# Both FFN products by one level of Strassen's seven half-size products, in two phases with the gated result parked in DRAM

## The chip, the cores and the metric

The kernel runs on one core of a Trainium2 chip. Its time is the device time of one execution in microseconds (us); before the change it is 1385.53 us, the median of three runs (1383.79 to 1386.12).

## The reference

One layer of an encoder on 1024 tokens of width 1024, in float32: a mixer (neighbourhood attention and gated linear attention) and then the part that the change touches, a gated feed-forward network (FFN) with a short convolution over the tokens, between two RMS norms:

```python
    h = h + rmsnorm(mix, norm_mix_post)
    a = rmsnorm(h, norm_ffn_pre) @ w_ffn_in
    half = CONV_W // 2
    ap = jnp.pad(a, ((0, 0), (half, half), (0, 0)))
    a = sum(ap[:, j:j + L] * conv_w[j] for j in range(CONV_W)) + conv_b
    val, gate = a[..., :D_FF], a[..., D_FF:]
    y = (jax.nn.gelu(gate, approximate=True) * val) @ w_ffn_out
    return h + rmsnorm(y, norm_ffn_post)
```

CONV_W is 3, D_FF 2816. The 16 rows of learned tokens ahead of the 1024 are dropped at the end. The first product is 1024 tokens x 1024 x 5632, the second 1024 x 2816 x 1024.

## The kernel before

The mixer takes the first 620 us; it is the same in both kernels. Every float32 operand of a large product is split in two parts of a shorter type: `split` (L146 to L148) makes `hi` with a cast on ScalarE and `lo = src - hi` on VectorE. A product is then three matmuls, hi x hi, hi x lo and lo x hi, added in PSUM.

How the FFN gets its input: the mixer's last step, for each of eight tiles of 128 tokens, adds the residual (L812), norms (L817) and transposes the result; `to_u2` (L832) splits it into `u2h` and `u2l`, features on the partitions, 8 chunks x 1026 token columns. The steps of this part stand in lists by name (T2, T3: `wt`, `ul`, `fr`), so the eighth tile is the last.

`ffn_in(j)`, for 22 blocks j of 128 value and 128 gate features: load 512 KB of weights for each half (L933), split them (L942, L943), and for three token pieces (344, 344 and 342 columns) and both halves, 24 matmuls (8 chunks of the width x 3: L954, L955, L957). ScalarE and VectorE take the piece out of PSUM through the convolution (L960, L963, L966), ScalarE does the gelu (L971), VectorE multiplies (L972), and the product is split into `yh`, `yl` (L147, L148), which stay in SBUF. The 512 KB of the second product's weights for this j are loaded and split too (L975).

`ffn_out(g)` multiplies the y of a group of 2 blocks (4 in the last) by their output weights: for 8 token tiles x 2 halves of 512 columns, 3 matmuls per block (L1006 to L1008), and VectorE adds the PSUM tile to `acc` (L1012). Group g-1 runs behind the first `ffn_in` of group g, so TensorE always has a product whose operands are there. The last `ffn_out` also norms each token tile: squares on ScalarE (L1015), a multiplication by the gain on POOL (L1021), the power on POOL, then VectorE's scaling and residual (L1034) and the store (L1035).

The order of the instructions on each engine is made by the tile framework's scheduler, within what the tiles' buffers allow; each engine then works through its own queue in that order. All loads and stores named here are issued by SP, in one queue.

## Time and profile before

| | |
|---|---|
| median of 3 runs | 1385.53 us |
| profiled execution | 1385.94 us, its span 1383.9 us |
| mean granted TensorE clock | 0.984 of full |
| TensorE (PE) busy | 97% of the span |
| VectorE (DVE) | 55% |
| ScalarE (ACT) | 37% |
| GpSimd (POOL) | 12% |
| DMA moved | 128.61 MB, mean 93 GB/s |

The times of all runs are of the whole program. The span is that of one profiled execution, from its first to its last instruction. "PE" is the matmuls, "PEld" the loading of weights into TensorE, which goes beside them. Matmuls are pipelined: the duration of one in the profile is longer than the distance to the next.

### The profile page before, as it was taken

The page shows a single profiled execution, that of the slowest core. Times are in us where ns is not written, and L with a number is a line of the kernel's source. Part 1 is how long each engine was busy: PE and PEld are TensorE (multiplying, and loading weights), DVE is VectorE, ACT ScalarE, POOL GpSimd, SP SyncE. Part 2 cuts the span into 40 slices and gives each one's busy share as a digit, 9 for nine tenths or more (in the row PEclk, how much of TensorE's full clock was granted, in tenths as well). Part 3 has the DMA queues.
Part 4 walks back from the last instruction along what each step waited for, and adds up shares of the span by engine and source line. Part 5 has one row for each costly group of instructions (what it writes and reads, how often), then busy time and mean ns, then how long its engine had stood idle before and what let it go on. Part 6 is the DMA issues. An engine that isn't in the chain of part 4 may idle for free.

```text
span 1383.9 us, 21562 instructions
## 1 busy us (share of the span) xinstructions
PE 1339.1 (97%) x8640; PEld 1209.0 (87%) x8642; DVE 760.2 (55%) x1445; ACT 517.3 (37%) x998; POOL 160.3 (12%) x242
## 2 busy tenths in 40 slices
PE   7979999999899899998999999999999999999998
PEld 6869888889788678778989898989898989898996
DVE  5491455545255667667555555555555555555545
ACT  5443534522245655545413132313141413141422
POOL 1170000000122335320000000000000000000025
PEclk9989999999999899998999999999999999999999
DMA  5311122212867965434201010111111111010222
GB/s 199 116 39 46 48 80 85 69 61 67 279 184 214 283 198 179 142 128 155 83 31 62 31 62 31 62 34 58 46 47 47 48 44 61 32 62 31 92 77 107
DMA packets 73474, 128.61 MB, mean 93 GB/s; under 512 B 13856, under 2 KB 46976, under 8 KB 73376
## 3 DMA queue, kind: packets, MB, share of 16 engines
q1 hardware_dynamic: 73376, 127.25, 28.3%
q8 instruction: 68, 1.11, 0.3%
q14 instruction: 30, 0.25, 0.1%
HBM read 105.27 MB, written 31.59 MB: 99 GB/s over the span
## 4 chain that ended last, share of the span: by engine, by line
PE 92%; DMA 3%; DVE 2%; ACT 1%; issue 0%; POOL 0%; SPq 0%; DVEq 0%; POOLq 0%; ACTq 0%
PE fi L954 12%; PE fi L955 12%; PE fi L957 12%; PE fo L1008 6%; PE fo L1007 6%; PE fo L1006 6%; PE ops L686 2%; PE wo L753 2%; PE wo L755 2%; PE pna L174 2%; PE wo L754 2%; PE pna L175 2%; PE pna L176 2%; PE pp L680 2%; PE pvn L187 1%; PE pvn L188 1%
## 5 line engine op out<-in xcount | busy, mean ns | idle before, releaser
L954 PE MATMUL fi<-u2h,fh 128*128 128x344 f32 (+1 forms) x1056 | 334.0, 321 | 0.7 <-ACT u2h L147 0.7
L955 PE MATMUL fi<-u2l,fh 128*128 128x344 f32 (+1 forms) x1056 | 334.5, 320 | 0.0
L954 PEld LDWEIGHTS fi<-u2h,fh 128*128 128x128 f32 x1056 | 199.2, 189 | 3.1 <-ACT u2h L147 1.1
L955 PEld LDWEIGHTS fi<-u2l,fh 128*128 128x128 f32 x1056 | 199.3, 189 | 1.9
L957 PE MATMUL fi<-u2h,fl 128*128 128x344 f32 (+1 forms) x1056 | 192.0, 319 | 0.0
L957 PEld LDWEIGHTS fi<-u2h,fl 128*128 128x128 f32 x1056 | 171.3, 188 | 1.9
L1012 DVE TENSOR_TENSOR acc<-fo,acc 128x512 f32<-128x512 f32 (+1 forms) x145 | 99.4, 686 | 101.9 <-PE fo L1008 100.7
L960 ACT ACTIVATE cv<-fi,vec 128x342 f32<-128x342 f32 x132 | 83.9, 636 | 190.8 <-PE fi L957 190.1
L963 DVE SCALAR_TENSOR_TENSOR cv<-fi,vec,cv 128x342 f32<-128x342 f32 x132 | 75.4, 571 | 129.4 <-ACT cv L960 128.9
L1008 PE MATMUL fo<-wol,yh 128*128 128x512 f32 (+1 forms) x356 | 139.5, 392 | 0.0
L1007 PE MATMUL fo<-woh,yl 128*128 128x512 f32 (+1 forms) x356 | 139.0, 390 | 0.0
L1006 PE MATMUL fo<-woh,yh 128*128 128x512 f32 (+1 forms) x356 | 138.6, 389 | 0.0
L147 ACT CAST woh<-wor 128x1024 fp32r<-128x1024 f32 x30 | 31.3, 1047 | 200.7 <-PE fo L1007 170.9
L1021 POOL TENSOR_TENSOR acc<-acc,g_po 128x512 f32<-128x512 f32 x15 | 21.9, 1463 | 720.5 <-ACT jk L1015 720.5
L1008 PEld LDWEIGHTS fo<-wol,yh 128*128 128x128 f32 x356 | 66.9, 188 | 14.3
L966 DVE SCALAR_TENSOR_TENSOR cv<-fi,vec,cv 128x342 f32<-128x342 f32 x132 | 75.5, 572 | 4.0
L1006 PEld LDWEIGHTS fo<-woh,yh 128*128 128x128 f32 x356 | 66.9, 188 | 12.2
L1007 PEld LDWEIGHTS fo<-woh,yl 128*128 128x128 f32 x356 | 66.9, 188 | 12.1
L174 PE MATMUL pna<-uh,wna_h 128*128 128x272 f32 (+2 forms) x192 | 63.9, 333 | 4.5 <-DVE qsl L148 4.5
L943 DVE TENSOR_TENSOR fl<-fr,fh 128x1024 fp32r<-128x1024 f32 x44 | 53.8, 1223 | 22.8 <-PE fi L957 18.7
L175 PE MATMUL pna<-ul,wna_h 128*128 128x272 f32 (+2 forms) x192 | 64.5, 336 | 0.0
L176 PE MATMUL pna<-uh,wna_l 128*128 128x272 f32 (+2 forms) x192 | 63.1, 328 | 0.0
(309 smaller groups left out, 2598.3 us busy)
## 6 DMA issues: line engine op xcount, KB each, us to landing
fr<-in_w_ffn_in_dram SPq DMA_DIRECT2D x44, 512.0 KB
wor<-in_w_ffn_out_dram SPq DMA_DIRECT2D x22, 512.0 KB
vt<-vw_d SPq DMA_DIRECT2D x16, 288.0 KB
xt<-in_x_dram SPq DMA_DIRECT2D x8, 512.0 KB
wna_r<-in_w_in_b_dram SPq DMA_DIRECT2D x8, 512.0 KB
wor<-in_w_o_dram SPq DMA_DIRECT2D x8, 512.0 KB
xr<-in_x_dram SPq DMA_DIRECT2D x8, 512.0 KB
h_d<-xr SPq DMA_DIRECT2D x8, 512.0 KB
```

Source lines behind the costliest of these rows:

```text
L174: mm(ps[:m, :n], wh, uh[:, k, t0 : t0 + n], start=(k == 0), stop=False)
L175: mm(ps[:m, :n], wh, ul[:, k, t0 : t0 + n], start=False, stop=False)
L176: mm(ps[:m, :n], wl, uh[:, k, t0 : t0 + n], start=False, stop=(k == KC - 1))
L954: mm(ps[:, :m], hi[:, k, :], u2h[:, k, t0 : t0 + m], start=(k == 0), stop=False)
L955: mm(ps[:, :m], hi[:, k, :], u2l[:, k, t0 : t0 + m], start=False, stop=False)
L957: mm(ps[:, :m], lo[:, k, :], u2h[:, k, t0 : t0 + m], start=False, stop=(k == KC - 1))
L960: nc.scalar.activation(c[:, :n], ps[:, 1 : n + 1], AF.Identity, bias=col(VEC_CB + ch), scale=col(VEC_CONV + 2 * NFC + ch))
L966: nc.vector.scalar_tensor_tensor(c[:, :n], ps[:, 2 : n + 2], col(VEC_CONV + 4 * NFC + ch), c[:, :n], ALU.mult, ALU.add)
L1006: mm(ps[:, :w], yh[:, tk], wh[:, cs], start=(x == 0), stop=False)
L1007: mm(ps[:, :w], yl[:, tk], wh[:, cs], start=False, stop=False)
L1008: mm(ps[:, :w], yh[:, tk], wl[:, cs], start=False, stop=(x == len(items) - 1))
L1012: nc.vector.tensor_tensor(acc[:, i, cs], ps[:, :w], acc[:, i, cs], ALU.add)
```

## The change

One level of Strassen's method (in Winograd's form) on both products: each operand is cut into 2 x 2 blocks, sums and differences of blocks are made, and seven block products take the place of eight. The two products no longer run in turns.

Phase 1, the first product. `to_u2` now only copies into `u2r` (plain float32). Its blocks are 4 chunks of the width x 514 token columns (two overlapping halves, for the convolution). Seven A operands (a11, a12, a22 and four sums) are made once: `a_sum` and one in-place subtraction, four operations of 2056 columns on VectorE, and `a_split`, seven casts on ScalarE and seven subtractions on VectorE, of 2056 columns too. For each j, `prep(j)` loads the same 2 x 512 KB of weights, makes four block differences of 512 columns on POOL, and splits seven operands of 512 columns (`b_split`). `prod(j, op, ...)` is one block product: 24 matmuls of 258 columns into a PSUM tile of two banks; X, Y and Z, three such tiles per j out of four buffers, collect the products 1+2, 6+7+4 and 5+3, and five VectorE adds of 516 columns into c21, c12 and c22 make the sums in between. Then come four convolutions, two gelus and two products of 512 columns. y goes to a DRAM tensor, `y_d`, 512 KB for each j.

Phase 2, the second product: seven sweeps (p7, p5, p6, p4, p3, p1, and the last product joined to p1's PSUM) of 11 k x 4 token tiles x 3 matmuls of 512 columns. Operands come in halves of 256 KB from `y_d` and from the output weights; sums of y are made on POOL, sums of weights on VectorE (op4: POOL), and each operand is split when its sweep needs it (rings of three). `e12`, `e21`, `e22` collect the quadrants in SBUF. `finish` is the norm, gain, residual and store; the first four tiles finish behind p1, the others during the last sweep.

The program also gets a smaller scratch memory for DMA descriptors (1024), which leaves more room in SBUF.

```diff
-            split(u2["h"][:, kk, c0 : c0 + P], u2["l"][:, kk, c0 : c0 + P], ptv)
+            if hf:
+                nc.vector.tensor_copy(u2["r"][:, kk, c0 : c0 + P], ptv)
+            else:
+                nc.scalar.copy(u2["r"][:, kk, c0 : c0 + P], ptv)
...
+    def b_split(j, op, src):
+        hi = fb.tile([P, 4, P], F32R, tag="bh", name=f"bh{j}_{op}", bufs=9)
+        nc.scalar.copy(hi, src)
+        lo = fb.tile([P, 4, P], F32R, tag="bl", name=f"bl{j}_{op}", bufs=9)
+        nc.vector.tensor_tensor(lo, src, hi.bitcast(F32), ALU.subtract)
...
+        nc.gpsimd.tensor_sub(f[5], b12, b11)
+        nc.gpsimd.tensor_sub(f[6], b22, f[5])
+        nc.gpsimd.tensor_sub(f[7], b22, b12)
+        nc.gpsimd.tensor_sub(f[4], b21, f[6])
...
+        for t in range(2):
+            c = slice(256 * t, 256 * t + 258)
+            for k in range(4):
+                mm(ps[:, t, :258], hi[:, k, :], ah[:, k, c], start=(first and k == 0), stop=False, skip_group_check=True)
+                mm(ps[:, t, :258], hi[:, k, :], al[:, k, c], start=False, stop=False, skip_group_check=True)
+                mm(ps[:, t, :258], lo[:, k, :], ah[:, k, c], start=False, stop=(k == 3), skip_group_check=True)
...
+    for j in range(NFC):
+        X = acc1[j, "x"]
+        c21, c12, c22 = evac("c21", j), evac("c12", j), evac("c22", j)
+        y = fc.tile([P, 4, 256], F32, tag="y", name=f"y{j}", bufs=2)
+        nc.scalar.copy(c21, X[:, :, :258])
+        prod(j, 6, "y", True)
+        Y = acc1[j, "y"]
+        prod(j, 2, "x", False)
+        nc.vector.tensor_add(c12, Y[:, :, :258], c21)
+        prod(j, 5, "z", True)
+        Z = acc1[j, "z"]
+        conv(j, 0, X, y[:, 0:2])
+        prod(j, 7, "y", False)
+        nc.vector.tensor_add(c22, Y[:, :, :258], c21)
+        nc.vector.tensor_add(c22, Z[:, :, :258], c22)
+        if 1 <= j < NFC - 1:
+            prep(j + 1)
+            prod(j + 1, 1, "x", True)
+        prod(j, 4, "y", False)
+        nc.vector.tensor_add(c21, Y[:, :, :258], c21)
+        prod(j, 3, "z", False)
+        nc.vector.tensor_add(c12, Z[:, :, :258], c12)
+        conv(j, 0, c21, y[:, 2:4])
+        gated(j, 1, c22, y[:, 2:4])
+        gated(j, 0, c12, y[:, 0:2])
+        nc.sync.dma_start(y_d[j], y.rearrange("p a b -> p (a b)"))
...
+    def sweep(name, operands):
+        ps = banks(name)
+        for k in range(NK):
+            A, B = operands(k)
+            for t in range(4):
+                mac(ps[t], A, B, t, k == 0, k == NK - 1)
+        return ps
...
+    def op7(k):
+        dload("yb", yb, k, yd(k, h1))
+        dload("ya", ya, k, yd(k, h0))
+        dload("wb", wb, k, wd_(k, h1))
+        dload("wc", wc, k, wd_(NK + k, h1))
+        s3, t3 = half("s3", f"s3_{k}", 2), half("t3", f"t3_{k}", 2)
+        nc.gpsimd.tensor_sub(s3, ya[k], yb[k])
+        nc.vector.tensor_tensor(t3, wc[k], wb[k], ALU.subtract)
+        return fsplit("a", k, 7, s3), fsplit("b", k, 7, t3)
...
+    def op5(k):
+        dload("yc", yc, k, yd(NK + k, h1))
+        dload("wa", wa, k, wd_(k, h0))
+        nc.gpsimd.tensor_add(yb[k], yb[k], yc[k])
+        nc.vector.tensor_tensor(wb[k], wb[k], wa[k], ALU.subtract)
+        return fsplit("a", k, 5, yb[k]), fsplit("b", k, 5, wb[k])
...
+    def op6(k):
+        nc.gpsimd.tensor_sub(yb[k], yb[k], ya[k])
+        nc.vector.tensor_tensor(wb[k], wc[k], wb[k], ALU.subtract)
+        return fsplit("a", k, 6, yb[k]), fsplit("b", k, 6, wb[k])
...
+    Q = sweep("p6", op6)
+    for t in range(4):
+        for e in (e21, e22, e12):
+            nc.vector.tensor_add(e[t], Q[t], e[t])
...
+            if i < 4 and hf == 0:
+                nc.vector.tensor_mul(dst, src, g_po[:, cs])
+            else:
+                nc.gpsimd.tensor_mul(dst, src, g_po[:, cs])
...
+    nc = _bacc.Bacc("TRN2", target_bir_lowering=False, num_devices=1, dynamic_dma_scratch_size=1024)
```

Three places where the order of an engine's instructions differs. First VectorE where the FFN begins, from the row that writes the eighth tile's `un`. Before (`fl` is the low part of a weight, `u2l` of the tokens, `cv` the convolution):

```order
L817 SCALAR_TENSOR_TENSOR un2_8_6870<-xr8_6949,rsb8_r_6970,g_norm_ffn_pre_5168 128x1024
L943 TENSOR_TENSOR fl1_0_7255<-fr1_0_7252,fh1_0_7254 128x1024
L148 TENSOR_TENSOR u2l_6753<-pt3_3_1_6983,u2h_6752 128x4x128
L148 TENSOR_TENSOR u2l_6753<-pt3_7_0_6990,u2h_6752 128x4x128
L148 TENSOR_TENSOR u2l_6753<-pt3_7_1_6997,u2h_6752 128x4x128
L148 TENSOR_TENSOR u2l_6753<-pt3_5_0_7006,u2h_6752 128x4x128
L963 SCALAR_TENSOR_TENSOR cv0_0_0_7085<-fi0_0_0_7060,vec_120,cv0_0_0_7085 128x342
```

Now, from the fifth operation on A operands (`al4` is the low part of operand 4, `as7` a sum, `bl1_2` the low part of weight operand 2 of j=1, `c120` is c12 of j=0):

```order
L150 TENSOR_TENSOR al4_7186<-u2r_6756,ah4_7185 128x2056
L150 TENSOR_TENSOR al5_7176<-as5_7167,ah5_7175 128x2056
L150 TENSOR_TENSOR al6_7172<-as6_7169,ah6_7171 128x2056
L906 TENSOR_TENSOR bl1_2_7121<-fr1_0_7099,bh1_2_7119 128x512
L906 TENSOR_TENSOR bl1_5_7125<-bt1_5_7107,bh1_5_7123 128x512
L978 TENSOR_TENSOR as7_7179<-u2r_6756 128x2056
L987 TENSOR_TENSOR as6_7169<-u2r_6756,as6_7169 128x2056
L906 TENSOR_TENSOR bl1_7_7129<-bt1_7_7109,bh1_7_7127 128x512
L906 TENSOR_TENSOR bl1_4_7133<-bt1_4_7110,bh1_4_7131 128x512
L150 TENSOR_TENSOR al7_7182<-as7_7179,ah7_7181 128x2056
L150 TENSOR_TENSOR al3_7191<-as6_7169,ah3_7190 128x2056
L1021 TENSOR_TENSOR c120_7200<-q0_y_7204,c210_7199 128x516
```

The first operation on a product, which before stood behind pieces of 512 columns, now stands behind all eleven of 2056 and four weight splits; op7 of j=0 waits for it.

Second, SP's queue where phase 1 ends. Before, the last loads of weights stand one behind the other, and then those of the residual (`hr`):

```order
L975 DMA wor2_20_12518<-in_w_ffn_out_dram 128x1024
L933 DMA fr21_1_12530<-in_w_ffn_in_dram 128x1024
L933 DMA fr21_0_12524<-in_w_ffn_in_dram 128x1024
L975 DMA wor2_21_12724<-in_w_ffn_out_dram 128x1024
L993 DMA hr1_12732<-h_d_99 128x1024
```

Now:

```order
L1038 DMA y_d_61<-y18_11457 128x1024
L1038 DMA y_d_61<-y19_11697 128x1024
L1038 DMA y_d_61<-y20_11937 128x1024
L1038 DMA y_d_61<-y21_12177 128x1024
L1086 DMA yb0_12375<-y_d_61 128x512
L1086 DMA ya0_12377<-y_d_61 128x512
L1086 DMA wb0_12379<-in_w_ffn_out_dram 128x512
L1086 DMA wc0_12381<-in_w_ffn_out_dram 128x512
```

The loads of phase 2, those of weights too, stand behind the store of the last y, which waits for that y.

Third, VectorE in the sweep p5 (`wb` are weights in place, L1102 for op5, L1107 already for op6; `al5`, `bl5` the low parts for op5). There is no such place before: its second product took splits that `ffn_in` had left behind.

```order
L1102 TENSOR_TENSOR wb2_12443<-wb2_12443,wa2_12789 128x512
L1107 TENSOR_TENSOR wb0_12379<-wc0_12381,wb0_12379 128x512
L1102 TENSOR_TENSOR wb3_12475<-wb3_12475,wa3_12815 128x512
L150 TENSOR_TENSOR bl5_1_12772<-wb1_12411,bh5_1_12771 128x512
L150 TENSOR_TENSOR bl5_2_12798<-wb2_12443,bh5_2_12797 128x512
L1102 TENSOR_TENSOR wb4_12507<-wb4_12507,wa4_12841 128x512
L150 TENSOR_TENSOR al5_2_12794<-yb2_12439,ah5_2_12793 128x512
L1107 TENSOR_TENSOR wb1_12411<-wc1_12413,wb1_12411 128x512
```

Four two-input operations stand here for each k of p5, one of them for the sweep after it.

## Rows read from the trace of the kernel before

**Rows 1.** The page: busy time of each engine, and the chain that ended last, by engine.

```profile
PE 1339.1 (97%) x8640; PEld 1209.0 (87%) x8642; DVE 760.2 (55%) x1445; ACT 517.3 (37%) x998; POOL 160.3 (12%) x242
...
PE 92%; DMA 3%; DVE 2%; ACT 1%; issue 0%; POOL 0%; SPq 0%; DVEq 0%; POOLq 0%; ACTq 0%
```

**Rows 2.** Matmuls by line and shape: count | busy us, mean ns | idle before.

```profile
L954 PE MATMUL fi<-u2h,fh 128*128 128x344 f32 x704 | 223.0, 321 | 0.7 <-ACT u2h L147 0.7
...
L1006 PE MATMUL fo<-woh,yh 128*128 128x512 f32 x348 | 136.4, 392 | 0.0
```

**Rows 3.** TensorE's timeline: start, duration (us); first and last of three even stretches.

```profile
200.75 0.28 PE L176 MATMUL pna<-uh,wna_l 128*128 128x256 f32 x1
...
202.17 0.28 PE L176 MATMUL pna<-uh,wna_l 128*128 128x256 f32 x1
...
203.24 0.39 PE L175 MATMUL pna<-ul,wna_h 128*128 128x512 f32 x1
...
207.17 0.39 PE L174 MATMUL pna<-uh,wna_h 128*128 128x512 f32 x1
...
1006.44 0.32 PE L954 MATMUL fi<-u2h,fh 128*128 128x344 f32 x1
...
1008.81 0.32 PE L955 MATMUL fi<-u2l,fh 128*128 128x344 f32 x1
```

**Rows 4.** Timeline at the FFN's start and end: last `wo`, last `un`, last `fo`.

```profile
619.78 0.40 PE L755 MATMUL wo<-wol,mh 128*128 128x512 f32 x1
...
631.88 1.28 DVE L817 SCALAR_TENSOR_TENSOR un<-xr,rsb_r,g_norm_ffn_pre 128x1024 f32<-128x1024 f32 x1 [0.66 <-POOL rsb_r L143]
...
1377.04 0.28 PE L1008 MATMUL fo<-wol,yh 128*128 128x256 f32 x1
```

**Rows 5.** Windows: us, busy of PE, PEld, DVE, ACT, POOL, PEclk, DMA share, GB/s.

```profile
620.00:632.00 12.00, 6.32 (x29) 4.97 (x28) 9.12 (x16) 5.64 (x12) 1.30 (x3) 0.64 0.87 306
...
646.00:1372.00 726.00, 726.00 (x4133) 682.20 (x4132) 398.48 (x637) 214.27 (x350) 21.66 (x19) 1.00 0.17 55
...
551.00:561.00 10.00, 10.00 (x79) 7.88 (x74) 7.70 (x23) 6.77 (x21) 4.93 (x9) 1.00 0.87 328
```

**Rows 6.** Splits by line and shape: count | busy us, mean ns | idle before.

```profile
L943 DVE TENSOR_TENSOR fl<-fr,fh 128x1024 fp32r<-128x1024 f32 x44 | 53.8, 1223 | 22.8 <-PE fi L957 18.7 <-ACT fh L942 3.7
...
L148 DVE TENSOR_TENSOR u2l<-pt,u2h 128x512 fp32r<-128x512 f32 x16 | 10.7, 685 | 5.8 <-ACT u2h L147 5.8
...
L147 ACT CAST mh<-mgl 128x512 fp32r<-128x512 f32 x8 | 4.9, 626 | 4.1 <-PE wo L755 4.1
```

**Rows 7.** Timeline of VectorE and POOL, operations of 512 columns, alone and together.

```profile
622.53 1.28 DVE L148 TENSOR_TENSOR u2l<-pt,u2h 128x512 fp32r<-128x512 f32 x2
...
611.86 1.41 DVE L812 SCALAR_TENSOR_TENSOR xr<-un,rsa_r,xr 128x512 f32<-128x512 f32 x2 [0.66 <-POOL rsa_r L143]
...
577.65 2.44 DVE L812 SCALAR_TENSOR_TENSOR xr<-un,rsa_r,xr 128x512 f32<-128x512 f32 x2
577.85 1.70 POOL L806 TENSOR_TENSOR un<-un,g_norm_mix_post 128x512 f32<-128x512 f32 x1 [1.46 <-ACT jk L805]
...
618.93 1.28 POOL L806 TENSOR_TENSOR un<-un,g_norm_mix_post 128x512 f32<-128x512 f32 x1 [3.47 <-ACT jk L805]
```

**Rows 8.** TensorE's timeline behind a wait in the mixer.

```profile
98.33 0.59 PE L176 MATMUL pg<-uh,wg_l 128*128 128x272 f32 x1 [7.50 <-DVE wg_l L148]
...
98.95 0.43 PE L175 MATMUL pg<-ul,wg_h 128*128 128x272 f32 x1
...
100.54 0.43 PE L176 MATMUL pg<-uh,wg_l 128*128 128x272 f32 x1
```

**Rows 9.** A 512 KB weight load: its issue, and the cast that waited for it.

```profile
620.21 0.33 SPq L906 DMA_DIRECT2D fr<-in_w_ffn_in_dram  x1
...
625.28 1.04 ACT L942 CAST fh<-fr 128x1024 fp32r<-128x1024 f32 x1 [2.51 <-DMA fr<-in_w_ffn_in_dram]
```

**Rows 10.** VectorE's last operations.

```profile
1379.40 1.42 DVE L1034 SCALAR_TENSOR_TENSOR acc<-acc,r_end,hr 128x512 f32<-128x512 f32 x2 [0.44 <-POOL r_end L1025]
```

More of the change, by code (lines that the diff above doesn't have):

```diff
@@ L1037, with a_split @@
-    groups = [(2 * g, 2 * g + 1) for g in range(9)] + [(18, 19, 20, 21)]
-    pend = None
-    for g, js in enumerate(groups):
-        items = [ffn_in(js[0])]
-        if pend is not None:
-            ffn_out(g - 1, pend, False)
-        items += [ffn_in(j) for j in js[1:]]
-        pend = items
-    ffn_out(len(groups) - 1, pend, True)
+    psum_s.close()
+    fas = ExitStack()
+    fa = fas.enter_context(tc.tile_pool(name="fa", bufs=1))
+    HC = 2 * 256 + 2
+    aops = {}
+    def a_split(op, src):
+        hi = fa.tile([P, 4, HC], F32R, name=f"ah{op}")
+        lo = fa.tile([P, 4, HC], F32R, name=f"al{op}")
+        split(hi, lo, src)
+        aops[op] = (hi, lo)
@@ new lines, with prod @@
+    a11, a12 = u2r[:, :4, :HC], u2r[:, 4:, :HC]
+    a21, a22 = u2r[:, :4, HC - 2 :], u2r[:, 4:, HC - 2 :]
+    a_split(1, a11)
+    a_split(2, a12)
+    ps1s = ExitStack()
+    ps1 = ps1s.enter_context(tc.tile_pool(name="ps1", bufs=1, space=bass.MemoryType.PSUM))
+    acc1 = {}
+    def prod(j, op, key, first):
+        if first:
+            acc1[j, key] = ps1.tile([P, 2, 512], F32, tag="q", name=f"q{j}_{key}", bufs=4)
+        ps = acc1[j, key]
+        hi, lo = wts.pop((j, op))
+        ah, al = aops[op]
+        for t in range(2):
[4 more added lines that the diff above has]
+                mm(ps[:, t, :258], lo[:, k, :], ah[:, k, c], start=False, stop=(k == 3), skip_group_check=True)
@@ new lines, with a_sum @@
+    prod(0, 1, "x", True)
+    prep(1)
+    prod(1, 1, "x", True)
+    fts = ExitStack()
+    ft = fts.enter_context(tc.tile_pool(name="ft", bufs=1))
+    def a_sum(op, x, y, alu):
+        t = ft.tile([P, 4, HC], F32, tag="as", name=f"as{op}", bufs=2)
+        nc.vector.tensor_tensor(t, x, y, alu)
+        return t
+    s1 = a_sum(5, a21, a22, ALU.add)
+    s2 = a_sum(6, s1, a11, ALU.subtract)
+    a_split(6, s2)
+    a_split(5, s1)
+    a_split(7, a_sum(7, a11, a21, ALU.subtract))
+    a_split(4, a22)
@@ new lines, in gated, with evac @@
+    def gated(j, half, src, val):
+        g = fc.tile([P, 2, 256], F32, tag="g", name=f"g{j}_{half}", bufs=3)
+        conv(j, 1, src, g)
+        nc.scalar.activation(g, g, AF.Gelu_apprx_tanh)
+        nc.vector.tensor_mul(val, val, g)
+    def evac(name, j):
+        return fc.tile([P, 2, 258], F32, tag=name, name=f"{name}{j}", bufs=2)
+    for j in range(NFC):
[24 more added lines that the diff above has]
+        nc.sync.dma_start(y_d[j], y.rearrange("p a b -> p (a b)"))
@@ new lines, with half, ring, banks @@
+    fcs.close()
+    fas.close()
+    fbs.close()
+    ps1s.close()
+    NK = NFC // 2
+    H = 512
+    ps2 = ctx.enter_context(tc.tile_pool(name="ps2", bufs=1, space=bass.MemoryType.PSUM))
+    fo = ctx.enter_context(tc.tile_pool(name="fo", bufs=1))
+    def half(tag, name, bufs=NK, dt=F32):
+        return fo.tile([P, H], dt, tag=tag, name=name, bufs=bufs)
+    def ring(tag, name):
+        return half(tag, name, 3, F32R)
+    h0, h1 = slice(0, H), slice(H, 2 * H)
+    def banks(name):
+        return [ps2.tile([P, H], F32, tag="o", name=f"{name}{t}", bufs=8) for t in range(4)]
@@ new lines, in fsplit, with mac @@
+    def fsplit(tag, k, op, src, lo=None, hi=None):
+        hi = ring(f"{tag}h", f"{tag}h{op}_{k}") if hi is None else hi
+        lo = ring(f"{tag}l", f"{tag}l{op}_{k}") if lo is None else lo
+        split(hi, lo, src)
+        return hi, lo
+    def mac(ps, A, B, t, first, last):
+        tk = slice(t * P, t * P + P)
+        mm(ps, A[0][:, tk], B[0], start=first, stop=False, skip_group_check=True)
+        mm(ps, A[1][:, tk], B[0], start=False, stop=False, skip_group_check=True)
+        mm(ps, A[0][:, tk], B[1], start=False, stop=last, skip_group_check=True)
@@ new lines @@
+    e12, e21, e22 = ([half(n, f"{n}_{t}", 4) for t in range(4)] for n in ("e12", "e21", "e22"))
+    Q = sweep("p7", op7)
+    for t in range(4):
+        nc.scalar.copy(e21[t], Q[t])
+    Q = sweep("p5", op5)
+    for t in range(4):
+        nc.scalar.copy(e12[t], Q[t])
+        nc.vector.tensor_add(e22[t], Q[t], e21[t])
+    Q = sweep("p6", op6)
+    for t in range(4):
+        for e in (e21, e22, e12):
+            nc.vector.tensor_add(e[t], Q[t], e[t])
+    Q = sweep("p4", op4)
+    for t in range(4):
+        nc.vector.tensor_add(e21[t], Q[t], e21[t])
@@ L1048, in _blocked @@
+    for t in range(4):
+        finish(4 + t, (e21[t], e22[t]), False)
+    for t in range(4):
+        for k in range(NK):
+            mac(R[t], o2[k][0], o2[k][1], t, False, k == NK - 1)
+        finish(t, (R[t], e12[t]), t == 3)
 def _blocked(w, c0, n):
```

235 lines of the change are left out of this document (98 added, 137 removed).

## The prediction, as it was put on record before the changed kernel ran

> **What bounds the kernel now.** I read the page first. TensorE is busy for 97% of the span, and 92% of the chain that ended last are its matmuls [rows 1]. Then the groups of instructions by shape [rows 2]: the first FFN product (`fi`) is 3168 matmuls of 342 to 344 columns, the second (`fo`) 1044 of 512 and 24 of 256. What one costs is not its own duration, since neighbours overlap, but the distance from start to start in TensorE's timeline [rows 3]. From the first to the last row of each pair: 12 steps of 256 columns in 1.42 us, 0.118 each; 15 steps of 344 in 2.37, 0.158; 17 steps of 512 in 3.93, 0.231. I use 0.1575 for the mix of 342 and 344. So the FFN's matmuls are 3168 x 0.1575 + 1044 x 0.2312 + 24 x 0.118 = 743.2 us of work. They stand between the last `wo` matmul, which ends at 620.2, and the last `fo` matmul, at 1377.3 [rows 4], 757.1 us: only 13.9 us are lost, nearly all before 632, where TensorE is busy for 6.3 of 12 us at a mean clock of 0.64; afterwards it is busy throughout at a clock of 1.00 [rows 5]. The other engines are idle for nearly half of that. So fewer TensorE columns are worth their full time, as long as what feeds and empties TensorE keeps up.
>
> The sum is made against the profiled execution: span 1383.9, time 1385.9, so time is span plus 2.0; the median of the runs, 1385.5, is 0.4 below that. About 0.2% (2.8 us) is what a measurement of this kernel can tell from no change.
>
> **TensorE's work: -88.7 us.** Phase 1 has 22 j x 7 products x 24 = 3696 matmuls of 258 columns. Between the steps for 256 and for 344 [rows 3] that is 0.1193 each: 440.9 us against 499.0. Phase 2 has 7 sweeps x 132 = 924 of 512: 213.6 against 244.2. Together 654.5 for 743.2.
> The Trainium skill, "TensorE: Matmul & The Clock Gate", section "Back-to-back issue gap", gives sustained spacings that grow far slower than the columns (81 ns at 128, 131 at 512), by which shorter matmuls would save little. The trace disagrees: 118 at 256 and 231 at 512.
>
> **The start: +15.7 (bounds +6 and +25).** Before, the FFN began on the first token columns while the last were being made. Now every A operand needs all of `u2r`, which needs the eighth token tile; its `un` is written at 631.9 to 633.2 [rows 4]. The change takes two `fl` subtractions (2.4 us) off VectorE's queue ahead of it; with transposes and copies (1.5 us) `u2r` is whole at 632. Then VectorE has 11 operations of 2056 columns. From 0.685 us for 512 columns and 1.223 for 1024 [rows 6] one is 2.3, 2.25 back to back. `al6` is the seventh of them: 647.7. Behind it stand four weight splits of 0.6 and four big operations before `c120`, for which op7 of j=0 waits: 659.5. Five products (14.3 us of TensorE) are done by then, so it is as if TensorE ran densely from 645.2. I add 2.5 for one wait in j=1, where a PSUM slot comes back late, and 2 for the clock: after 7.5 us of idleness seven steps of 272 columns take 0.227 us each, nearly twice the warm price [rows 8]. That makes 649.7, or 29.5 lost, against 13.9. The lower bound has VectorE's order fully overlapped, the upper one all 11 operations (25 us) ahead of the dense stretch.
>
> **Steady phase 1: +3 (bounds 0 and +38).** One j is 168 x 0.1193 = 20.0 us of TensorE. VectorE has 22 operations in it: 14 of 0.60 to 0.69 (a lone split takes 0.685, a pair 1.28 [rows 6, 7]) and 8 of 0.66 to 0.71 (a pair takes 1.41 [rows 7]), 13.7 to 15.4. POOL has 4 subtractions of 1.28. These collide: the same pair of VectorE operations takes 2.44 instead of 1.41 when a POOL multiplication starts in it, which itself takes 1.70 [rows 7]. So each POOL operation costs VectorE up to 1.03: 17.8 to 19.5, still under 20.0. ScalarE has 14 operations of 0.6 to 0.8, under 11. Walked through VectorE's queue for one period, the add into `c22` that frees Y for op4 has some 3 us of slack, because op1 of j+1 stands between. So TensorE stays the bound; I take 3 us of small waits, 1 of them in j=21, where no op1 is left to cover. What covers this is op1; without it every j would stop for about 3 us.
>
> **Between the phases: +11.5 (bounds 9 and 18).** Nothing of before shows this wait, so I build it. SP issues the first load of phase 2 behind the store of y21, and that store waits for the last gated product. From the last matmul of phase 1: the `c12` add 0.7, convolution 0.8 and 1.4, gelu 0.6, multiplication 0.7, handovers, 4.7 in all. Then four issues of 0.33 [rows 9] and four halves landing, 1 MB: the same queue's 512 KB issued at 620.2 gave its cast at 625.3 [rows 9] with other loads beside it, and 328 GB/s is the best stretch of 10 us [rows 5], so 4.2 for the pair that the first subtraction needs and what is issued before it; then the POOL subtraction 1.3, cast 0.6 and split 0.7: 11.5. Lower bound: landing in 2. Upper: landing of all four in 6, and later splits late. Before, nothing stopped here, since SP always had the next loads ahead.
>
> **Phase 2: +17.7 (bounds +5 and +30).** A sweep is 132 x 0.2312 = 30.5 us. In p7 each k needs four halves, 1.05 MB: at 328 GB/s 3.2 us, where TensorE needs 2.78, 11 x 0.42 = 4.6 us, and the clock is cold after the wait (some 3 us by [rows 8], partly at the same time): +4. p5 is the worst: the scheduler has put op6's subtractions of VectorE into it too, so 44 two-input operations of 0.60 and 16 of POOL that cost 1.03 each, 42.9 against 30.5, less 2.4 us that the rings of 3 are ahead: +10. From p6 to p4, 12 adds of `e` tiles (7.3 us) stand ahead of the splits for k=2, with 4.8 to 5.6 of cover: +2.5. The rest 1.2. Between bounds far apart I stand near the row that shows the collision.
> The Trainium skill ("SBUF — State Buffer", section "Who interferes with whom") calls that collision an exclusive lock on a shared port pair, taken by two-input operations of VectorE. The rows agree. A hold over all of POOL's 1.28 would make p5 47 us, an estimate by that page, and my sum 4 us longer.
>
> **The tail: +2.4 (bounds 0 and +6).** Now 6.6 us from the last matmul [rows 4] to the end, where VectorE's last two operations start at 1379.4 [rows 10]. POOL is now given 20 additions and multiplications of 1.28 with powers between, 28 us in a sweep of 30.5, so the last tile queues behind a little: 9.
>
> **Sum:** -88.7 + 15.7 + 3 + 11.5 + 17.7 + 2.4 = -38.4: span 1345.5, and with the 2.0 around it 1347.5; I say **1347**.
>
> Costed at nothing: the weight loads and stores of y in phase 1, 1.5 MB per j or 75 GB/s, and the smaller scratch memory, which only makes room.
>
> **The rivals.**
> - Better cover (0.08): splits of p5 keep ahead, phase 2 costs 5 instead of 17.7 (12.7 less), start and wait between the phases at their lower bounds (9.7 and 2.5 less): 25 us less, 1322. For it: POOL is busy for 22 of 726 us now [rows 5], so little collides elsewhere. Against: the rings hold three operands only.
> - The collision binds phase 1 too (0.12): a period of 21.2 to 21.8 instead of 20.0, 21 x 1.2 to 1.8 = 25 to 38 more: 1372 to 1385. For it: the high ends above sum to 19.5, and VectorE runs in order.
> - VectorE's in-order queue becomes phase 1's bound (0.07), **slower**: 15.4 us unpacked, POOL's four at full 1.28 (5.1) and about 2 of handovers from ScalarE make 22.5 a period, 21 x 2.5 = +53: 1400. It turns to a loss from 38.4 / 21 = 1.8 us of waiting per j. Against it: VectorE is busy for 398 of 726 us now [rows 5], half of the time, and the handovers are part of what the slack of 3 us above covers.
> - The shorter matmuls don't save (0.03): at the 344-column price phase 1's work would be 582 us, +141, 1488; slower. It would take a floor per instruction or a weight load that shows, and the 256-column row [rows 3] shows neither. The Trainium skill's spacings cited above would mean this.
>
> **How the numbers follow.** Forecast 0.70, better cover 0.08, phase 1 touched 0.12, the two slower ones 0.07 and 0.03. The predicted time is the forecast's, 1347. The range goes from the better cover, 1322, to the lower end of phase 1's collision, 1376: it leaves out the two slower cases and most of that one. Faster by over 0.2%: the first three less a little of the collision's upper end, 0.89; within 0.2%: 0.01; slower 0.10.
>
> **What would show it.** Right: starts of 258-column matmuls 0.119 apart; 20 to 20.2 us from j to j; idleness of TensorE before p7 of 10 to 13 us, released by a load; p5 some 10 us longer than 30.5 with VectorE's splits as releasers; TensorE's first dense stretch from about 660. Wrong: waits of TensorE in every j that VectorE ends, periods over 20.5, or a wait between the phases over 18.

## The result, and the profile after

The changed kernel takes 1365.22 us, the median of four runs (1363.30 to 1366.30), against 1385.82 for the kernel before beside it: a ratio of 0.9842, 95% interval 0.9806 to 0.9877. It is 20.6 us faster, where 38 were forecast; the time lies inside the forecast range. Its profiled execution has a span of 1363.1 us against 1383.9.

The page of the changed kernel: busy time by engine, and the chain that ended last by engine (the counterparts of [rows 1]).

```profile
PE 1265.5 (93%) x9024; PEld 1132.7 (83%) x9026; DVE 924.6 (68%) x1525; ACT 609.3 (45%) x1138; POOL 391.7 (29%) x389
...
PE 76%; DVE 10%; DMA 7%; issue 2%; POOL 2%; ACT 2%; SPq 1%; DVEq 0%; POOLq 0%; ACTq 0%
```

TensorE lost its hold on the end: 76% of the chain instead of 92%, with VectorE and the transfers in its place. Where, the windows show (us, busy time of PE, PEld, DVE, ACT and POOL, clock, DMA share, GB/s; as [rows 5]): a piece of phase 1, then the sweeps p7, p5, p6, p4, p3, p1 and the last one.

```profile
800.00:1000.00 200.00, 200.00 (x1670) 200.00 (x1669) 152.90 (x219) 90.42 (x140) 59.15 (x40) 1.00 0.23 80
1115.50:1151.20 35.70, 33.67 (x132) 25.64 (x133) 33.50 (x35) 14.05 (x24) 18.65 (x13) 0.94 1.04 382
1151.20:1197.60 46.40, 35.22 (x133) 26.14 (x132) 46.40 (x42) 16.05 (x30) 32.68 (x20) 0.93 0.30 112
1197.60:1228.90 31.30, 30.45 (x134) 24.63 (x133) 26.01 (x32) 14.59 (x26) 18.88 (x12) 1.00 0.03 9
1228.90:1260.30 31.40, 30.22 (x133) 24.69 (x132) 27.39 (x33) 17.98 (x32) 14.02 (x11) 1.00 0.27 84
1260.30:1290.20 29.90, 29.90 (x133) 24.77 (x132) 24.90 (x41) 17.82 (x32) 0.00 (x0) 1.00 0.30 97
1290.20:1320.20 30.00, 30.00 (x134) 24.82 (x134) 19.70 (x32) 11.48 (x21) 0.54 (x1) 1.00 0.00 1
1320.20:1349.80 29.60, 29.60 (x132) 24.53 (x131) 23.22 (x28) 10.77 (x30) 29.60 (x24) 1.00 0.32 107
```

In this piece of phase 1 TensorE never stops: 1670 matmuls in 200 us, 0.120 apart. A sweep without waits takes 29.9 us, 0.2267 per matmul. p7 has the DMA engines full (1.04, 382 GB/s) and takes 35.7. p5 has VectorE busy for all of its 46.4 us, with 42 operations that back to back take 0.60 us each, and POOL busy for 32.7 us of the same stretch.

The waits of TensorE in this kernel, from the FFN on (in total, times, longest):

```profile
PE p L1068 <- ACT bh L149: 16.7, 3, 15.4
PE q_x L965 <- ACT c L1017: 8.3, 1, 8.3
PE p L1069 <- DVE al L150: 7.5, 7, 2.7
PE p L1070 <- DVE bl L150: 6.2, 2, 4.8
```

The first is the wait between the phases, the second stands in the start, the last two in phase 2. Before, TensorE's longest wait after 615 us was one of 3.0 us:

```profile
PE pt L832 <- DVE u2l L148: 5.0, 3, 3.0
```

The start, in VectorE's and then ScalarE's timeline (start, duration, operation): from the last piece of `u2r` to the first add into c12.

```profile
637.26 0.69 DVE L836 COPY u2r<-pt 128x512 f32<-128x512 f32 x1 [2.06 <-PE pt L834]
638.06 2.30 DVE L978 TENSOR_TENSOR as<-u2r 128x2056 f32<-128x2056 f32 x1
...
649.12 4.50 DVE L150 TENSOR_TENSOR al<-as,ah 128x2056 fp32r<-128x2056 f32 x2
...
660.37 4.50 DVE L150 TENSOR_TENSOR al<-as,ah 128x2056 fp32r<-128x2056 f32 x2
665.52 0.70 DVE L1021 TENSOR_TENSOR c<-q_y,c 128x516 f32<-128x516 f32 x1 [0.66 <-ACT c L1017]
...
664.90 1.08 ACT L1017 COPY c<-q_x 128x516 f32<-128x516 f32 x2 [3.51 <-DVE al L150]
```

`u2r` is whole at 637.95. The eleven operations, with four weight splits between them, fill VectorE from there to 664.87. ScalarE stood idle for 3.5 us before it could copy the first c21, and only then could op2 of j=0 start, at 665.5, with four products done.

The wait between the phases and the end: SP's queue, then VectorE, POOL and TensorE.

```profile
1107.95 0.32 SPq L1086 DMA_DIRECT2D yb<-y_d  x1
...
1104.43 0.69 DVE L1008 TENSOR_TENSOR y<-y,g 128x512 f32<-128x512 f32 x1 [0.70 <-ACT g L1007]
1114.10 0.69 DVE L1095 TENSOR_TENSOR t<-wc,wb 128x512 f32<-128x512 f32 x1 [8.97 <-DMA wc<-in_w_ffn_out_dram]
...
1111.87 1.26 POOL L1094 TENSOR_TENSOR s<-ya,yb 128x512 f32<-128x512 f32 x1 [57.75 <-DMA ya<-y_d]
...
1099.89 0.28 PE L967 MATMUL q_z<-ah,bl 128*128 128x258 f32 x1
1115.54 0.77 PE L1068 MATMUL p<-bh,ah 128*128 128x512 f32 x1 [15.38 <-ACT bh L149]
...
1349.85 0.39 PE L1070 MATMUL p<-w2l,y2h 128*128 128x512 f32 x1
...
1358.25 1.41 DVE L1181 SCALAR_TENSOR_TENSOR of<-of,rsc_r,hr 128x512 f32<-128x512 f32 x2 [0.73 <-POOL rsc_r L145]
```

The last y is ready at 1105.1, the first load goes out at 1107.95, the fourth has landed at 1114.1. The last matmul ends at 1350.2, 12.9 us before the end of the span.

### The profile page after: what moved, and what is told of

Its sections match the earlier page's. It is cut to its first block, busy times and chain, and to the rows that moved or that the text cites. A ratio compares the mean times of both kernels' runs of the same rounds, so it can differ in the third digit from the quotient of the medians.

```text
span 1363.1 us, 23186 instructions
## 1 busy us (share of the span) xinstructions
PE 1265.5 (93%) x9024; PEld 1132.7 (83%) x9026; DVE 924.6 (68%) x1525; ACT 609.3 (45%) x1138; POOL 391.7 (29%) x389
## 4 chain that ended last, share of the span: by engine, by line
PE 76%; DVE 10%; DMA 7%; issue 2%; POOL 2%; ACT 2%; SPq 1%; DVEq 0%; POOLq 0%; ACTq 0%
PE q_y L965 5%; PE q_y L967 5%; PE q_y L966 5%; PE q_z L965 3%; PE q_z L967 3%; PE q_z L966 3%; PE q_x L965 3%; PE q_x L966 3%; PE q_x L967 3%; PE p L1069 3%; PE p L1070 3%; PE p L1068 3%; DMA wb<-in_w_ffn_out_dram 2%; PE ops L688 2%; PE pna L176 2%
## 5 line engine op out<-in xcount | busy, mean ns | idle before, releaser
L965 PE MATMUL q_y<-ah,bh 128*128 128x258 f32 x528 | 149.1, 283 | 0.8 <-DVE c L1026 0.8
L967 PE MATMUL q_y<-ah,bl 128*128 128x258 f32 x528 | 148.9, 282 | 0.0
L966 PE MATMUL q_y<-al,bh 128*128 128x258 f32 x528 | 148.9, 282 | 0.0
L1069 PE MATMUL p<-bh,al 128*128 128x512 f32 x264 | 105.4, 403 | 7.5 <-DVE al L150 7.5
L965 PE MATMUL q_x<-ah,bh 128*128 128x258 f32 x352 | 101.3, 288 | 10.3 <-ACT c L1017 8.3
L966 PE MATMUL q_x<-al,bh 128*128 128x258 f32 x352 | 101.3, 288 | 2.6 <-DVE al L150 2.6
L967 PE MATMUL q_x<-ah,bl 128*128 128x258 f32 x352 | 101.0, 287 | 0.0
L965 PEld LDWEIGHTS q_y<-ah,bh 128*128 128x128 f32 x528 | 99.6, 189 | 1.0 <-DVE c L1026 1.0
L965 PE MATMUL q_z<-ah,bh 128*128 128x258 f32 x352 | 99.9, 284 | 0.0
L967 PEld LDWEIGHTS q_y<-ah,bl 128*128 128x128 f32 x528 | 99.7, 189 | 0.0
L906 DVE TENSOR_TENSOR bl<-bt,bh 128x512 fp32r<-128x512 f32 x88 | 73.9, 843 | 27.6 <-ACT bh L904 27.6
```

What stands on the lines that cost most here:

```text
L906: nc.vector.tensor_tensor(lo, src, hi.bitcast(F32), ALU.subtract)
L965: mm(ps[:, t, :258], hi[:, k, :], ah[:, k, c], start=(first and k == 0), stop=False, skip_group_check=True)
L966: mm(ps[:, t, :258], hi[:, k, :], al[:, k, c], start=False, stop=False, skip_group_check=True)
L967: mm(ps[:, t, :258], lo[:, k, :], ah[:, k, c], start=False, stop=(k == 3), skip_group_check=True)
L1069: mm(ps, A[1][:, tk], B[0], start=False, stop=False, skip_group_check=True)
```

## The experiments

Each kernel was timed beside the kernel before on the same chip. The intervals of the ratios are 0.16% to 0.36% wide to either side, 2 to 5 us, so for parts of a few us the length of a stage in the trace decides. The stages are counted from the last `wo` matmul or from the moment `u2r` is whole, because the mixer, whose instructions are the same, ended between 618.8 and 627.3 us in these profiles. For the changed kernel they are: `wo` to `u2r` 19.1, `u2r` to the end of phase 1 462.2, wait 15.4, p7 35.7, p5 46.4, p6 31.3, p4 31.4, tail 12.9. The runs that leave the start alone (1, 2, 3, 6 and 7) have 19.0 to 19.6 and 462.0 to 463.1 in the first two; differences smaller than that say nothing.

**1. y in 22 DRAM tensors**

```diff
-    y_d = dram.tile([NFC, P, SEQ], F32, name="y_d")
+    y_d = [dram.tile([P, SEQ], F32, name=f"y_d{j}") for j in range(NFC)]
```

> y in DRAM as 22 tensors instead of one, so that the first load of phase 2 reads a y that was stored long ago. In the changed kernel TensorE stands still for 15.4 us between the phases, and the first load is issued at 1107.95, just after the last store has landed (1105.15 plus 2.61). Theory A (the load waits because the store of y21 writes the same DRAM tensor): the load is issued some 2.5 us earlier, 1362.5 to 1363 in all. Theory B (it waits for SBUF, because the memory of phase 2 is that of the y tile, which the store still reads): no change, 1364 to 1366, and the wait stays 15 us.

Measured: 1368.39, ratio 0.9864 (0.9839 to 0.9889). The wait between the phases is 16.5 us, not shorter. SP's first load again goes out 7.8 us behind the end of phase 1 (1104.2 there; 1100.2 and 1107.95 in the changed kernel):

```profile
1112.01 0.32 SPq L1086 DMA_DIRECT2D yb<-y_d  x1
```

So theory A fell. What is left is SBUF: the memory of phase 2 lies over that of phase 1, and the load's wait covers the store that still reads y21, which in the changed kernel's chain lands at 1107.76:

```profile
1105.15 2.61 DMA y_d<-y
```

That SBUF is the cause rests on A's fall. Run 7 fits it: its first load into phase 2's memory again goes out 7.8 us behind the end of phase 1. Its loads into phase 1's own memory went out before that, but they also stand ahead of the last store in SP's queue, so they don't settle it.

**2. The sums of y on VectorE**

```diff
-        nc.gpsimd.tensor_add(yb[k], yb[k], yc[k])
+        nc.vector.tensor_add(yb[k], yb[k], yc[k])
...
-        nc.gpsimd.tensor_sub(yb[k], yb[k], ya[k])
+        nc.vector.tensor_sub(yb[k], yb[k], ya[k])
```

> The sums of y for op5 and op6 (22 operations) on VectorE instead of POOL. In the changed kernel the sweep p5 takes 46.4 us, where its matmuls need 29.9. Theory A (each POOL operation in it holds VectorE up for about 1.1 us, more than the 0.60 that the same operation costs on VectorE): VectorE then has some 66 operations of 0.60 in p5, 40 us, and the whole gets 5 to 8 us faster, 1357 to 1360. Theory B (VectorE's number of operations, or the rings of three, bind p5, and POOL's operations are hidden): 22 more operations of 0.60 on VectorE make it up to 13 us slower, 1365 to 1378.

Measured: 1359.42, ratio 0.9794 (0.9762 to 0.9826). p5 fell from 46.4 to 38.8 us and p6 from 31.3 to 29.9, with 22 more operations on VectorE: theory A. First p5 in the changed kernel, VectorE and POOL:

```profile
1152.45 1.78 DVE L150 TENSOR_TENSOR al<-yb,ah 128x512 fp32r<-128x512 f32 x1
1154.16 1.77 DVE L1102 TENSOR_TENSOR wb<-wb,wa 128x512 f32<-128x512 f32 x1
...
1157.02 5.07 POOL L1101 TENSOR_TENSOR yb<-yb,yc 128x512 f32<-128x512 f32 x3
```

and then VectorE in p5 of this run, and its window:

```profile
1173.53 0.68 DVE L150 TENSOR_TENSOR al<-yb,ah 128x512 fp32r<-128x512 f32 x1
1174.13 0.68 DVE L1101 TENSOR_TENSOR yb<-yb,yc 128x512 f32<-128x512 f32 x1
...
1155.00:1193.80 38.80, 32.89 (x133) 25.54 (x133) 38.80 (x65) 15.52 (x29) 2.65 (x1) 0.96 0.41 149
```

In the changed kernel's p5 the two engines, where they meet, go in step, one operation each in 1.7 us; without POOL VectorE does one every 0.60. A POOL operation there thus costs VectorE 1.1 us to save it 0.60. Now VectorE's own 65 operations x 0.60 = 39 us set p5, still 9 more than TensorE needs.

**3. The tail on VectorE**

```diff
-            if i < 4 and hf == 0:
-                nc.vector.tensor_mul(dst, src, g_po[:, cs])
-            else:
-                nc.gpsimd.tensor_mul(dst, src, g_po[:, cs])
+            nc.vector.tensor_mul(dst, src, g_po[:, cs])
...
-        for e, eng in ((e21, nc.vector), (e22, nc.gpsimd), (e12, nc.gpsimd)):
+        for e, eng in ((e21, nc.vector), (e22, nc.vector), (e12, nc.vector)):
```

> In the tail the two adds into e22 and e12 and all multiplications by the gain on VectorE, POOL left with the powers. The end now comes 12.9 us after the last matmul (6.6 before the change). Theory A (POOL's 20 operations of 1.26 and their collisions put the last tiles behind): 6 to 7 us after the last matmul, 1358 to 1360 in all. Theory B (VectorE's own queue is full): no gain or up to 3 us more.

Measured: 1362.19, ratio 0.9820 (0.9795 to 0.9845). The tail is 7.6 us instead of 12.9, a little over theory A's 6 to 7, and the whole is 2 us over A's 1360: the last matmul starts at 1352.72 and VectorE's last pair of operations at 1356.19, 3.5 us behind it instead of 8.4.

```profile
1356.19 1.42 DVE L1178 SCALAR_TENSOR_TENSOR of<-of,rsc_r,hr 128x512 f32<-128x512 f32 x2 [0.73 <-POOL rsc_r L145]
```

**4. The first c21 in its own memory**

```diff
+    fc0 = fas.enter_context(tc.tile_pool(name="fc0", bufs=1))
+    c21_0 = fc0.tile([P, 2, 258], F32, name="c21_0")
...
-        c21, c12, c22 = evac("c21", j), evac("c12", j), evac("c22", j)
+        c21, c12, c22 = evac("c21", j) if j else c21_0, evac("c12", j), evac("c22", j)
```

> The first c21 tile gets memory of its own. In the changed kernel ScalarE is idle for 3.5 us before the first c21 copy and TensorE for 8.3 us behind it, since that tile lies where the sums of A operands were, and they are read until 664.9. Theory A (memory holds the copy back): op2 of j=0 runs before 658, so that five instead of four products are done when op7 can start near 666: 3 to 4 us faster, 1361 to 1362. Theory B (the eleven operations on VectorE bind the start whatever c21 does, the next wait takes its place): under 1 us, 1364 to 1366.

Measured: 1364.87, ratio 0.9836 (0.9807 to 0.9864). Five products instead of four ran before the long wait, and `u2r` to the end of phase 1 is 461.1 instead of 462.2, between 1 and 2 us less. The wait of 8.3 us shrank to 6.9 and changed its name:

```profile
PE q_y L965 <- ACT y L998: 6.9, 1, 6.9
```

That is theory B's mechanism at a little more than its figure, and far from A's 3 to 4: the memory is a real wait, but another stood right behind it.

**5. The first j's block differences on VectorE**

```diff
-        nc.gpsimd.tensor_sub(f[5], b12, b11)
+        (nc.gpsimd if j else nc.vector).tensor_sub(f[5], b12, b11)
...
```

(and the other three in the same way)

> The four block differences of the first j's weights on VectorE instead of POOL. In the changed kernel the last token tile is whole in u2r 19.1 us after the last wo matmul; POOL's queue has those four differences (6 us with their stretching) between the norms of the last two tiles, and its multiplication for the eighth tile starts at 624.6. Theory A (they delay the eighth tile): u2r is whole about 3 us earlier, 16 us after the last wo matmul, and the whole is 2 to 4 us faster, 1362 to 1364 beside 1366. Theory B (the eighth tile waits for its matmuls and its own chain): u2r stays at 19 us, no change.

Measured: 1364.85, ratio 0.9861 (0.9841 to 0.9880); no gain in the whole can be told. `u2r` is whole 17.4 us after the last `wo` matmul, 1.7 earlier, half of theory A. In the changed kernel it was not the first j's differences that stood right ahead of POOL's multiplication for the eighth tile, as I had read it, but those of j=1, which POOL still makes there in this run:

```profile
621.35 1.26 POOL L921 TENSOR_TENSOR bt<-fr,bt 128x512 f32<-128x512 f32 x1
622.58 1.71 POOL L808 TENSOR_TENSOR un<-un,g_norm_mix_post 128x512 f32<-128x512 f32 x1
```

Run 8 has the same edit and takes 18.3 us, only 0.8 earlier; runs 10 and 12, with both j's differences on VectorE, take 16.6 and 16.1.

**6. POOL's work in phase 1 doubled**

```diff
+        for _ in range(2 if j > 1 else 1):
+            nc.gpsimd.tensor_sub(f[5], b12, b11)
...
```

> Every block difference of phase 1 is made twice on POOL from the third j on, eight operations per j instead of four; this adds work that is not needed. Theory A (as the prediction priced it, each POOL operation holds VectorE up by 1.03): VectorE needs 13.7 + 8 x 1.03 = 21.9 us per j and binds; the period goes from 20.15 to about 22, the whole 35 us slower, about 1400. Theory B (the trace of the changed kernel has VectorE busy for 15.4 us per j, so a POOL operation costs it some 0.4, as most of its partners there read PSUM): 17 us per j, the period stays at 20.15, under 3 us slower.

Measured: 1367.09, ratio 0.9869 (0.9849 to 0.9889), an interval that overlaps the changed kernel's; the period stays at 20.15 us and phase 1 takes 460.7 us from first to last matmul, 460.9 in the changed kernel. Theory B. The same window as above:

```profile
800.00:1000.00 200.00, 200.00 (x1670) 200.00 (x1669) 182.11 (x221) 86.90 (x140) 122.91 (x80) 1.00 0.23 80
```

VectorE is busy for 182 us instead of 153: 29 us for 40 more POOL operations, 0.7 each. Even at that price it stays inside TensorE's 200. Which operations stretch, the trace of the changed kernel shows in the same window: two kinds with both inputs in SBUF, L906 (up to 1.24 us, from 0.68) and L1008 (up to 1.13), by 11.6 us in all for 40 POOL operations, 0.3 each. The adds that read PSUM keep 0.68 to 0.70, the 18 of L1026 too that run beside a POOL operation between 700 and 1080 us.

```profile
L906 DVE TENSOR_TENSOR bl<-bt,bh 128x512 fp32r<-128x512 f32 x40 | 34.1, 852 | 14.1 <-ACT bh L904 14.1
...
L1026 DVE TENSOR_TENSOR c<-q_y,c 128x516 f32<-128x516 f32 x10 | 7.0, 696 | 8.4 <-PE q_y L967 8.4
```

**7. The first operands of p7 early**

```diff
+        if j == NFC - 1:
+            for k in range(NE):
+                early(k)
...
+    Q7 = banks("p7")
+    for k in range(NE):
+        for t in range(4):
+            mac(Q7[t], *e7[k], t, k == 0, False)
+    fbs.close()
```

`early(k)` loads the four halves into phase 1's weight buffers, subtracts and splits them there; NE is 2. y is in 22 tensors, and the raw halves of these k are loaded again in op5 and op6.

> y in 22 tensors, and the operands of p7 for k=0 and 1 are loaded, subtracted and split in phase 1's memory during j=21; their raw halves are loaded once more for later sweeps. Now TensorE stands still for 15.4 us before p7, and p7 takes 35.7 us with the DMA engines busy throughout. Theory A (the wait is the chain from the last y through SBUF's release to the loads, and p7 is then held by its loads): the wait before p7 falls to 1 to 2 us, about 10 us of wait then stand behind k=1, and p7 ends 8 to 10 us earlier, since nine loads of 1 MB stand where eleven did: 1356 to 1359 beside 1366. Theory B (p7 is bound by VectorE and POOL, which are busy for 33.5 of its 35.7 us): the wait moves behind k=1 and p7 ends at most 5 us earlier.

Measured: 1361.89, ratio 0.9831 (0.9812 to 0.9850). The wait before p7 fell to 0.9 us and one of 9.1 came up behind the early matmuls, as theory A had it:

```profile
PE p L1075 <- DMA wb<-in_w_ffn_out_dram: 9.1, 1, 9.1
```

From the end of phase 1 to the end of p7 it is 43.65 us instead of 51.04: p7 ends 7.4 earlier, between B's 5 and A's 8 to 10, nearer to A. But p6, where the second loading is needed, grew from 31.3 to 33.6, so 5 us are left. What binds the rest of p7 is open: behind that wait its nine k take 28.0 us with the DMA share at 1.04 again, and VectorE is busy for 25.4 of them.

**8. These five together**

The edits of runs 2, 3, 4, 5 and 7 in one kernel.

> The sums of y on VectorE, the tail on VectorE, the first c21 in its own memory, the first j's differences on VectorE and the early operands, all in one. If the parts add up, as places one behind the other should: 9 for the sums, 5 for the tail, 2 for c21, 3 for the first differences and 8 for the early operands, 27 us, 1339 beside 1366. If one wait takes the place of another, 1345 to 1355.

Measured: 1342.35, ratio 0.9697 (0.9674 to 0.9720). Each part kept its place: p5 36.8, tail 7.6, `u2r` to the end of phase 1 460.1, end of phase 1 to the end of p7 43.9, p6 33.8. Beside the ratio of the changed kernel it is 20 us faster, less than the 27 of the plain sum (1342 lies between the two cases that were expected); the terms that I had set too high are the early operands (8 for 5) and the first differences (3 for 0.8 in this run, where `u2r` takes 18.3).

**9. The sums of A operands in halves, in place**

```diff
+    ts = [ft.tile([P, 2, HC], F32, tag="as", name=f"as{i}", bufs=2) for i in range(2)]
+    for op, x, y, alu in ((5, a21, a22, ALU.add), (6, None, a11, ALU.subtract), (3, a12, None, ALU.subtract)):
+        for kk, t in zip(kks, ts):
+            nc.vector.tensor_tensor(t, t if x is None else x[:, kk], t if y is None else y[:, kk], alu)
+            a_low(op, kk, t)
...
```

> The sums of A operands are made in two halves of 1028 columns in two buffers, in place from one sum to the next, and the room this saves holds c21, c12 and y of j=0, so that nothing of j=0 but c22 waits for the memory of the sums. VectorE's work is the same to within 1 us. In the changed kernel four products are done 27.6 us after u2r is whole, when op2 of j=0 starts. Theory A (the memory of the sums held back the first products, VectorE's queue only their last): eight or nine products are done by then, phase 1 ends 9 to 13 us earlier after the last wo matmul (468 to 472 us instead of 481), 1353 to 1357 beside 1366. Theory B (VectorE's queue itself, in order, holds each product back): like the run with c21 alone, about 2 us.

Measured: 1369.51, ratio 0.9885 (0.9866 to 0.9903), but with the mixer's end at 627.3 us, 8 us later than in the changed kernel. `u2r` to the end of phase 1 is 461.1, 1.1 less. With j=0 free of the sums' memory, TensorE's longest wait there is for a convolution of j=0 that stands between the sums in VectorE's queue:

```profile
PE q_y L965 <- DVE y L1010: 3.6, 1, 3.6
```

Theory A fell.

**10. All, with the start of run 9 and four early k**

> The combined kernel with this start in place of c21's own memory, the differences of the first two j on VectorE, the operands of p7 for k=0 to 3 made early instead of 0 and 1, and the second loading of their raw halves for p6 moved behind the loads of p5. If each does what the runs before show of its kind: 8 us at the start, 4 to 6 at p7 (two more k cover the wait behind the early ones), 2 to 4 in p6, which took 33.8 with those loads and 29.9 without: 1324 to 1330 beside 1342. If p7 is bound by VectorE and POOL instead, 1331 to 1336.

Measured: 1338.66, ratio 0.9662 (0.9639 to 0.9684), the fastest kernel of the study, but slower than both ranges that were expected (1324 to 1330, and 1331 to 1336). p6 is back at 30.5 us and `u2r` comes 16.6 after the last `wo` matmul; `u2r` to the end of phase 1 takes 461.6, no better than in run 8 (460.1). With four early k the loads now wait for the early matmuls, and end of phase 1 to end of p7 is 42.0.

**11. Four low parts left out**

```diff
+        if op in (3, 4, 5, 7):
+            nc.scalar.copy(hi, src)
+            aops[op] = (hi, aops[1][1])
+            return
```

> It leaves out the low parts of A operands 3, 4, 5 and 7: their products read the low part of operand 1 instead, so four of VectorE's eleven operations of 2056 columns are gone and the matmuls keep their number. The run with c21 alone and the one with the sums in halves each moved the start by under 2 us. Theory A (VectorE's eleven operations, one behind the other, set the start): phase 1 ends 7 to 9 us earlier after u2r is whole (453 to 455 us instead of 462), some 1357 in all. Theory B (the waits are those of memory and PSUM buffers, whatever VectorE has to do): under 3 us.

Measured: 1359.79, ratio 0.9805 (0.9786 to 0.9825). `u2r` to the end of phase 1 is 453.6 us instead of 462.2: 8.7 less for four operations of 2.2. Theory A. The wait for the c21 copy is down to 1.1 us:

```profile
PE q_x L969 <- ACT c L1021: 1.1, 1, 1.1
```

This run also ends the reading of the sums' memory earlier, so it takes runs 4 and 9, which freed that memory without taking work off VectorE and gained 1.1 us each, to tell the two apart. Together they show that the start is VectorE's eleven operations, one behind the other; memory and PSUM buffers mostly decide which wait carries their name.

**12. Three early k**

The kernel of run 8 with the differences of the first two j on VectorE, NE = 3, and the second loading of `ya` and `wc` at the end of p5.

> The combined kernel with c21 in its own memory, the differences of the first two j on VectorE, three early k instead of two or four, and the second loading of their raw halves behind the loads of p5. With four early k the loads waited for the early matmuls, with two the matmuls for the loads; three lie where both come at about the same time. 1334 to 1339; if the start with the sums in halves was the better one, 1338 to 1342.

Measured: 1343.62, ratio 0.9694 (0.9678 to 0.9710), a miss. End of phase 1 to end of p7 is 43.2 us, p6 32.4, the tail 8.6: each 1 to 2 us worse than in run 10, while the start (460.4) and p5 (36.9 against 37.9) are each about 1 us better. Of the 4.5 us by which the profiled span is longer, 3.0 are the mixer's, which ended later. Why three k did not do better than two or four wasn't followed further.

## Why the prediction was right, and where it was short

The sign, the mechanism and the places were right: TensorE's work fell by what the step times said, and four places gave time back. Each of the four gave back more than its term. In the prediction's order, from the two profiled executions:

| term | forecast | measured | how |
|---|---|---|---|
| TensorE's work | -88.7 | -90.4 | 3696 x 0.11995 + 924 x 0.2267 = 652.8, against 743.2 |
| start | +15.7 | +23.0 | 618.9 to 1100.2 less 443.3 and 1.1: 36.9 lost, 13.9 before |
| steady phase 1 | +3 | +1.1 | one gap, in j=21; period 20.15 |
| between the phases | +11.5 | +15.4 | the wait before p7 |
| phase 2 | +17.7 | +25.2 | 234.7 less 209.5 |
| tail | +2.4 | +6.3 | 12.9, against 6.6 |
| the mixer's end | 0 | -1.3 | 618.9, against 620.2 |
| sum | -38.4 | -20.7 | spans: -20.8 |

**TensorE's work.** Right to 2 us. 258 columns cost 0.120, a hair over the interpolated 0.1193 (+2.4); 512 cost 0.2267 in the sweeps and not the 0.2312 of [rows 3] (-4.1). The rival that shorter matmuls don't save is refuted. The spacings of the Trainium skill ("TensorE: Matmul & The Clock Gate", section "Back-to-back issue gap"), 81 ns at 128 columns and 131 at 512, don't hold for these matmuls: 120 at 258, 227 at 512.

**The start.** The step that failed is "`u2r` is whole at 632", 11.8 us behind the last `wo` matmul: it was 637.95, 19.1 behind it. I took two subtractions off VectorE's queue and didn't count what the change puts on POOL's, the differences of j=0 and j=1 in the middle of the norms; moving them brought `u2r` forward by 1.7 and 0.8 us (j=0's alone, runs 5 and 8) and by 2.5 and 3.0 (both, runs 10 and 12). The chain from the last `un` to the last copy took 2.7 us where I had 1.5. By subtraction 3 to 4 of the 7.3 us are left; the 2.4 us that I had taken off for the two subtractions may be part of them, but no run shows it. The second part came out right in size, dense work as if from 655.8, 17.8 us behind `u2r`, where I had 17.7, but in part by luck: four products instead of five were done before the long wait (2.9 us more), and the wait in j=1 for which I had 2.5 didn't come. I had op7 waiting for c12 in VectorE's queue and missed that c21's memory is the sums' memory; run 4 took that away for 1 to 2 us, and runs 4, 9 and 11 show that the queue is what binds.

**Steady phase 1.** Right, and with more cover than claimed. I priced a POOL operation at up to 1.03 us of VectorE; it costs 0.3 there, by what VectorE's operations stretch, and 0.7 with twice as many (run 6); the adds that read PSUM did not stretch beside it. The rival of a collision that binds phase 1 needed far more than that. The slower rival, VectorE's queue as the bound, had its place and its mechanism in the wrong phase: it does bind, in p5 and at the start.

**Between the phases.** The 4.7 us to the last y were right (4.9). The step that failed is that SP's order alone holds the loads: they wait 2.8 us more, until the store has landed, for SBUF and not for the DRAM tensor (run 1). The pair for the first subtraction was there 3.9 us behind the first issue, where I had 4.2, but the wait ended with the weights' pair behind it, which was there after 6.2: I had followed the wrong pair.

**Phase 2.** The mechanism in p5 was right and its size too small: +16.5 where I had +10. VectorE, busy for all of p5, sets its length: 42 operations of 0.60 and 20 of POOL at 1.1 make 47. I had 16 of POOL at 1.03, and took off 2.4 us for the rings, which did not show. The Trainium skill ("SBUF — State Buffer", section "Who interferes with whom") calls the port pair that VectorE and POOL share an exclusive lock; the rows of p5, where each pair takes 1.7 us, agree that one engine's operation holds up the other's, and the hold is 1.1 us, less than POOL's whole 1.28. p7 lost 5.8 (4 forecast, though its own two terms were 4.6 and up to 3; the loads ran at 382 GB/s and not at 328), p6 and p4 2.9 (2.5 forecast, with another 1.2).

**The tail.** I saw POOL's 20 operations and gave them 2.4 us; they cost 5.3 of the 6.3 (run 3). That they hold VectorE back as in p5 I had not carried over to this place: near the end a pair of its operations takes 3.36 us, where the last pair takes 1.41.

```profile
1348.72 3.36 DVE L1181 SCALAR_TENSOR_TENSOR of<-of,rsc_r,hr 128x512 f32<-128x512 f32 x2
```

**The signs and the range.** Of the signs that I named, the steps of 258 columns (0.120) and the period (20.12 to 20.15) came as said; the wait before p7 (15.4 for 10 to 13), p5 (16.5 for some 10) and the stretch without stops (from 665.5 for about 660) each went past theirs. The range's upper end, 1376, is not the lower end of the collision's rival, which I had worked out as 1372; the time lies below both.

Worked out from the same numbers, not from a run of its own: the first product gained 55.7 us of work and gave back 24.1, the second gained 34.7 and gave back 46.9. As built, only the first pays. In run 10 the second gives back some 23: 0.9 before p7, 11.2 in it, 8.0 in p5, 2.0 in p6 and p4, 1.0 in the tail; there it pays too, by some 12.
